# A modulation vector's product moved from matmuls to vector sums, in a three-block model kernel on one Trainium2 core

## The chip, the cores and the metric

The kernel runs on one core of a Trainium2 chip as one program. The metric is the device time of one execution in microseconds (us). The engines spoken of are PE (TensorE, matmuls into PSUM), DVE (VectorE), ACT (ScalarE), POOL (GpSimd) and SP (SyncE, which here only issues the weight loads). Each runs its own queue of instructions in a fixed order and waits on semaphores of the others.

## The reference

All arithmetic is f32: 256 tokens, width 1024. The program is a chain of differential attention, a mixture of 64 experts, latent attention (MLA), another 64 experts, and a last block: a hybrid mixer (window attention "swa", forgetting attention "fox") and a convolutional gated MLP. The last block is modulated by six vectors of a second input `c`:

```python
mod = jax.nn.silu(c) @ w_ada + b_ada            # [1, 1024] @ [1024, 6144]
sh1, sc1, ga1, sh2, sc2, ga2 = jnp.split(mod, 6, axis=-1)
h = modulate(rms_norm_2(x, g_attn), sh1, sc1)   # h * (1 + sc1) + sh1
x = x + ga1[:, None, :] * hybrid_mixer(h, w_in, b_f, sinks, w_out)
h2 = modulate(rms_norm_2(x, g_mlp), sh2, sc2)
x = x + ga2[:, None, :] * conv_glu_mlp(h2, w_up, conv_w, conv_b, w_down)
return rms_norm_2(x, g_final)
```

The change concerns `silu(c) @ w_ada`: one row times 24 MB of weights.

## The kernel before, in words

The stages follow one another: differential attention (0 to 143 us of the profiled span), the first experts (143 to 600), MLA (to about 720), the second experts (to 1262), the mixer (to 1416), the MLP (to 1630). A list scheduler sets the order of every engine's queue when the program is built; SP's order is that of the code, and the experts' PE order is written by hand.

Weights go through 16 **regions** of SBUF (`Regions`), each a 128x2048 f32 tile of 1 MB. `make_plan` lists all loads in order; `fill` issues the next one on SP (L122) whenever a region is free, `done` frees a region after its last reader. So one region that is held longer delays the load that would take its place, and all loads behind it in the queue.

**Modulation.** `cs` (128x8) is silu(c), with k = 0..7 blocks of 128 rows in its columns. `Ada` (class at L429) works through the pieces of a part of `w_ada`. Parts 0 (sh1, sc1) and 1 (ga1, sh2) are 8 pieces of one k block and 2048 columns; parts 4 (sc2) and 5 (ga2) are 4 pieces of two k blocks and 1024 columns. For each k block four matmuls (L444) with a 128x32 broadcast column of `cs` as stationary operand add the four quarters of the columns into the four quadrants of a PSUM tile. These are f32 and each counts as two instructions in the trace: 64 for a part. When the last block is in, `finish` (L453) adds the bias (L462), and transposes (L466) and copies (L471) bring the vector to columns. Part 5 goes another way: ACT copies and POOL adds (L458, L459), and `gate_row` (L481) spreads the row over the partitions.

Part 0 is stepped at the end of differential attention, parts 1 and 4 two pieces at a time beside the mixer's projections qa, qb, kb, vb (`gemm_tok`, L514, through `beside`), part 5 at the end of the mixer's `out_proj` (L552). Its four loads stand in the plan directly behind the four of `w_out`, ahead of the MLP's.

**Around it.** `gemm_tok` and `out_proj` split each weight tile in two (`split`: ACT L399 makes the high part, DVE L400 the low part, 128x1024 each) and `mm3` multiplies in three passes (L415, L416, L417). L416 is the first that needs the low part. While Ada accumulates in PSUM (`ad_ps`), `gemm_tok` with `beside` leaves that tile out (`acc_ps(beside is None)`) and goes through three accumulators. In an attention's pipeline DVE does the score maxima (L586, L588), ACT the exponentials, PE the transposes (L596), and DVE the scaling (L738 in differential attention, L624 in swa). `fence` holds later work back behind the row norms.

Of the kernel before, what the change touches and what calls it, by code (L numbers as in the profile page):

```python
# [18 lines left out]
P = 128  # L19
T = 2  # L20
# [150 lines left out]
def make_plan(a, stop):  # L171
# [5 lines left out]
    def rows(name, w, ncol, k0, nk, c0, nc_):  # L177
        add(name, (nk, nc_), dram(w, k0 * P * ncol + c0, [[ncol, P], [P * ncol, nk], [1, nc_]]))
# [35 lines left out]
    for kh in range(4):  # L214
        rows(("mix_out", kh), a["w_out_2"], 1024, 2 * kh, 2, 0, 1024)
    ada = ada_plan(a, add, (5,))
    for _ in range(4):
        next(ada)
    for i in range(11):
        rows(("up", 0, i), a["w_up_2"], 2 * FF2, 0, 8, 256 * i, 256)  # L220
        rows(("up", 1, i), a["w_up_2"], 2 * FF2, 0, 8, FF2 + 256 * i, 256)
        rows(("down", i), a["w_down_2"], 1024, 2 * i, 2, 0, 1024)
    ends = {1: ("diff_out", 3), 2: ("moe", 0, 15, "d", 3), 3: ("mla_out", 3), 4: ("moe", 1, 15, "d", 3),
            5: ("mix_out", 3)}
    if stop in ends:
# [14 lines left out]
def tile_model(ctx: ExitStack, tc: tile.TileContext, a: dict, out: bass.AP, stop: int = 6):  # L240
# [45 lines left out]
    def acc_ps(four):  # L286

        turn[0] = (turn[0] + 1) % 4
        return ad_ps() if four and turn[0] == 0 else mm_ps()
# [139 lines left out]
    class Ada:  # L429


        def __init__(self, *parts, room=ad_ps):
            self.todo = [(s, pc) for s in parts for pc in ada_pieces(s)]
            self.room = room

        def step(self, n=1):
            for s, (key, k0, nk, _, ncol) in self.todo[:n]:
                if k0 == 0:
                    self.acc = self.room()
                w, m = reg.get(key), ncol // 4  # L440
                with behind_fence():
                    for k in range(nk):
                        for j in range(4):
                            PE.matmul(self.acc[32 * j:32 * j + 32, 0:m],  # L444
                                      lhsT=cs[:, k0 + k:k0 + k + 1].to_broadcast([P, 32]),
                                      rhs=w[:, k, m * j:m * j + m], start=(k0 + k == 0), stop=(k0 + k == 7))
                reg.done(key)
                if k0 + nk == 8:
                    self.finish(s, m)
            self.todo = self.todo[n:]  # L450

# [61 lines left out]

    def gemm_tok(hT, wkeys, ncol, evac, k0=0, beside=None):  # L514

        accs = [acc_ps(beside is None) for _ in range(T)]
        nk = sum(n for _, n in wkeys)
        k = 0
        for key, n in wkeys:
            w = reg.get(key)  # L520
            step = max(1, 1024 // ncol)
            for b in range(0, n, step):
                m = min(step, n - b)
                ws = split(w[:, b:b + m, :])
                for kk in range(m):
                    for t in range(T):
                        mm3(accs[t][:, :ncol], [z[:, k0 + k, ts(t, P)] for z in hT], [z[:, kk, :] for z in ws],
                            k == 0, k == nk - 1)
                    k += 1
            reg.done(key)  # L530
            if beside is not None:
                beside()
        for t in range(T):
            evac(t, accs[t][:, :ncol])

    def out_proj(oT, keys, vec=None):
        accs = token_accs()
        gate = None
        for kp in range(4):
# [8 lines left out]
                        mm3(accs[t][hf], [z[:, k, ts(t, P)] for z in oT], [z[:, ts(hf, 512)] for z in ws],  # L548
                            k == 0, k == 7)
            reg.done(keys[kp])  # L550
        if vec is not None:
            Ada(5, room=sc_ps).step(4)  # L552
        add_to_x(accs, gate)

    def add_to_x(accs, gate=None):
# [878 lines left out]
    def mlp(held):  # L1434
# [35 lines left out]
        def down(j):  # L1470
# [8 lines left out]
                        j == 0, j == NFF - 1)  # L1479
            if j2 == 1:  # L1480
                reg.done(("up", 0, i), ("up", 1, i), ("down", i))
        for j in range(NFF - 1):
            if j >= 2:
                down(j - 2)
            up(j)
        up(NFF - 1)
        for j in range(NFF - 3, NFF):
            down(j)
# [97 lines left out]
```

## Time and profile before

| | |
|---|---|
| median of 3 runs | 1635.39 us (1633.10 to 1638.16) |
| profiled execution, own time | 1631.57 us |
| its span in the trace | 1629.8 us |
| mean granted PE clock | 0.919 of full speed |
| busy: PE, DVE, ACT | 82%, 42%, 27% of the span |
| read from HBM | 508 MB |

The shares are means over stages with different limits, so the rows further down are read by stage: windows give what each engine does in a stretch, the timelines which instruction waits for what. Matmuls are pipelined: one row's time contains the end of the pipeline, and the distance between the starts of rows that follow one another is what an instruction takes from PE. Lines are those of the kernel before; in the changed one most are shifted by 7 to 9.

### The profile page before, as it was taken

The numbers are of one execution on the slowest core, as the hardware profiler recorded it, in microseconds if no ns is written. First come the engines' busy times: TensorE is split into PE (matmuls) and PEld (weight loads), VectorE is DVE, ScalarE is ACT, GpSimd is POOL, SyncE is SP. The second block draws the span as 40 slices with busy tenths as digits, with TensorE's granted clock in tenths as the row PEclk, the third lists the DMA queues.
The fourth block names the chain that finished last, engine by engine and source line by source line (L and its number), as shares of the span: only waits on it lengthen the run. The fifth ranks groups of instructions, "written<-read, shape, count | busy, mean of one in ns | idle before, by whom it ended". The sixth has DMA issues, their size and how long they took to land. (4 is left out here: it accounts for less than half of the span.)

```text
span 1629.8 us, 26706 instructions
## 1 busy us (share of the span) xinstructions
PE 1342.7 (82%) x10695; PEld 927.9 (57%) x10695; DVE 691.8 (42%) x1630; ACT 434.5 (27%) x946; POOL 54.1 (3%) x69
## 2 busy tenths in 40 slices
PE   7998987777677777998877677778777899999996
PEld 6766654443354444776643454545442656599996
DVE  6875232222222223775322222222322754477776
ACT  5764010000000001774000000000001543455555
POOL 2100000000000000120000000000000010000001
PEclk9998999889878899999988989899888999999998
DMA  9377889999999998244999999999899764475410
GB/s 365 127 262 322 334 343 419 419 419 418 417 397 416 418 418 337 93 144 167 392 417 403 418 419 418 419 418 393 341 418 379 285 235 159 149 270 189 171 37 27
DMA packets 112810, 513.14 MB, mean 315 GB/s; under 512 B 13955, under 2 KB 41283, under 8 KB 61344
## 3 DMA queue, kind: packets, MB, share of 16 engines
q1 hardware_dynamic: 111296, 508.14, 78.5%
q8 instruction: 160, 2.62, 0.7%
q0 software_dynamic: 1024, 1.41, 0.3%
q14 instruction: 106, 0.87, 0.1%
q10 hardware_dynamic: 224, 0.10, 0.0%
HBM read 508.56 MB, written 1.05 MB: 313 GB/s over the span
## 5 line engine op out<-in xcount | busy, mean ns | idle before, releaser
L955 PE MATMUL ad<-R,t 128*32 128x256 f32 x4352 | 327.0, 421 | 101.4 <-DMA R<-in_moe_w_up_dram 42.2
L955 PEld LDWEIGHTS ad<-R,t 128*32 128x32 f32 x4352 | 171.1, 120 | 260.3 <-issue 87.6
L910 PE MATMUL sc<-t,R 128*128 128x128 f32 x1120 | 176.1, 323 | 18.2 <-issue 12.0
L910 PEld LDWEIGHTS sc<-t,R 128*128 128x128 f32 x1120 | 167.5, 237 | 20.6 <-issue 17.2
L1007 DVE TENSOR_TENSOR x<-x,mm 128x512 f32<-128x512 f32 x140 | 90.0, 684 | 149.0 <-PE mm L1004 149.0
L982 PE MATMUL mm<-R,t 128*32 128x512 f32 x1120 | 135.4, 625 | 9.5 <-PEq L1047 5.0
L961 ACT ACTIVATE t<-ad 128x256 f32<-128x256 f32 x34 | 13.0, 383 | 481.7 <-PE ad L955 481.7
L963 DVE TENSOR_TENSOR t<-t,ad 128x256 f32<-128x256 f32 x34 | 14.3, 421 | 254.4 <-ACT t L961 254.4
L409 ACT ACTIVATE t<-mm,ws 128x512 fp32r<-128x512 f32 x64 | 44.0, 687 | 263.1 <-PE mm L982 263.1
L912 DVE TENSOR_TENSOR t<-sc,ffng 128x512 f32<-128x512 f32 x70 | 48.4, 692 | 134.6 <-PE sc L910 134.6
L400 DVE TENSOR_TENSOR R<-R,R 128x1024 fp32r<-128x1024 f32 (+3 forms) x78 | 93.2, 1198 | 27.4 <-ACT R L399 26.1
L400 DVE TENSOR_TENSOR t<-R,t 128x1024 fp32r<-128x1024 f32 (+3 forms) x76 | 88.7, 1171 | 23.6 <-ACT t L399 23.4
L410 DVE SCALAR_TENSOR_TENSOR t<-mm,ws,t 128x512 fp32r<-128x512 f32 x64 | 48.0, 751 | 104.3 <-ACT t L409 77.5
L399 ACT ACTIVATE R<-R 128x1024 fp32r<-128x1024 f32 (+3 forms) x78 | 78.7, 1014 | 50.8 <-PE ad L417 15.1
L934 PE MATMUL at<-con,t 128*128 128x128 f32 x70 | 16.6, 323 | 85.5 <-PEq L1083 73.9
L1004 PE MATMUL mm<-t,t 128*128 128x512 f32 x256 | 77.6, 422 | 11.1 <-DVE x L1007 10.2
L399 ACT ACTIVATE t<-R 128x1024 fp32r<-128x1024 f32 (+3 forms) x76 | 76.4, 1008 | 37.8 <-PE ad L416 15.3
L982 PEld LDWEIGHTS mm<-R,t 128*32 128x32 f32 x1120 | 35.0, 114 | 82.9 <-issue 77.5
L1004 PEld LDWEIGHTS mm<-t,t 128*128 128x128 f32 x256 | 43.1, 188 | 45.6 <-DVE x L1007 22.8
L934 PEld LDWEIGHTS at<-con,t 128*128 128x128 f32 x70 | 7.9, 155 | 99.7 <-issue 89.5
L415 PE MATMUL mm<-R,R 128*128 128x512 f32 (+3 forms) x139 | 56.4, 408 | 3.3 <-ACT R L399 2.6
L416 PE MATMUL mm<-R,R 128*128 128x512 f32 (+3 forms) x139 | 55.4, 399 | 0.0
(448 smaller groups left out, 2263.8 us busy)
## 6 DMA issues: line engine op xcount, KB each, us to landing
R<-in_moe_w_gate_dram SPq DMA_DIRECT2D x128, 1024.0 KB, 15.2
R<-in_moe_w_up_dram SPq DMA_DIRECT2D x128, 1024.0 KB, 15.8
R<-in_moe_w_down_dram SPq DMA_DIRECT2D x128, 1024.0 KB, 19.8
R<-in_w_ada_dram SPq DMA_DIRECT2D x24, 1024.0 KB, 7.7
R<-in_w_up_dram SPq DMA_DIRECT2D x22, 1024.0 KB, 6.3
R<-in_diff_w_in_dram SPq DMA_DIRECT2D x12, 1024.0 KB, 15.0
R<-in_w_down_dram SPq DMA_DIRECT2D x11, 1024.0 KB, 5.5
R<-in_w_in_dram SPq DMA_DIRECT2D x8, 1024.0 KB, 7.7
```

Of the source, the lines that this page charges most:

```text
L399: S.activation(hi, w, AF.Copy)
L400: V.tensor_tensor(lo, w, hi.bitcast(F32), op=ALU.subtract)
L409: first = S.activation(hi, src, AF.Copy, scale=scale)
L410: V.scalar_tensor_tensor(lo, src, scale, hi.bitcast(F32), op0=ALU.mult, op1=ALU.subtract)
L415: PE.matmul(acc, lhsT=lt[0], rhs=rt[0], start=start, stop=False, **kw)
L416: PE.matmul(acc, lhsT=lt[0], rhs=rt[1], start=False, stop=False, **kw)
L910: PE.matmul(pg[:, ts(k4, P)], lhsT=h[:, t, 4 * hb + k4, :], rhs=gm[:, t].rearrange("p a b -> p (a b)"), start=(t == 0), stop=(t == 1))
L912: V.tensor_tensor(xg[hb], pg.rearrange("p (k n) -> p k n", k=4), gain[:, 4 * hb:4 * hb + 4, None].to_broadcast([P, 4, P]), op=ALU.mult)
L955: mm = PE.matmul(pgu[32 * j:32 * j + 32, co:co + 256], lhsT=xg[k // 4][:, k % 4, 32 * j:32 * j + 32], rhs=w, start=(k == 0 and co == 0), s ...
L982: mm = PE.matmul(py[32 * j:32 * j + 32, :], lhsT=hT2[:, k, 32 * j:32 * j + 32], rhs=ws[j][:, k, ts(hf, 512)], start=(k == 0), stop=(k == 1))
L1004: PE.matmul(pos[t], lhsT=sc[:, ts(t, P)], rhs=y[part], start=(part == 0), stop=(part == 1))
L1007: V.tensor_tensor(xs, xs, pos[t], op=ALU.add)
```

## The change

For each k block of a part the 128 rows of weights stay in their partitions and are multiplied by the partition's own value of `cs`: ACT copies with a scale for k = 0 (new L447) and DVE adds `weights * cs + sum` for the others (new L449, `scalar_tensor_tensor`, 128x1024, in place into the region of the part's first piece). Where k = 1 stands in the first piece too (parts 4 and 5) it is added from there. After the last block four matmuls (new L455) against a vector of ones add the partitions, into a tile of `sc_ps`. Per 1024 columns that is one ACT copy and seven DVE additions: 42 additions and 6 copies in all. The first piece's region is freed only after these matmuls. `gemm_tok` always goes through four accumulators. Part 5's loads move in the plan behind the MLP's loads i = 1, 3, 5, 7, and its steps into the MLP's loop at j = 3, 7, 11, 15.

```diff
--- before.py
+++ after.py
@@ -214,12 +214,12 @@
     for kh in range(4):
         rows(("mix_out", kh), a["w_out_2"], 1024, 2 * kh, 2, 0, 1024)
     ada = ada_plan(a, add, (5,))
-    for _ in range(4):
-        next(ada)
     for i in range(11):
         rows(("up", 0, i), a["w_up_2"], 2 * FF2, 0, 8, 256 * i, 256)
         rows(("up", 1, i), a["w_up_2"], 2 * FF2, 0, 8, FF2 + 256 * i, 256)
         rows(("down", i), a["w_down_2"], 1024, 2 * i, 2, 0, 1024)
+        if i % 2:
+            next(ada)
     ends = {1: ("diff_out", 3), 2: ("moe", 0, 15, "d", 3), 3: ("mla_out", 3), 4: ("moe", 1, 15, "d", 3),
             5: ("mix_out", 3)}
     if stop in ends:
@@ -429,23 +429,32 @@
     class Ada:
 
 
-        def __init__(self, *parts, room=ad_ps):
+        def __init__(self, *parts):
             self.todo = [(s, pc) for s in parts for pc in ada_pieces(s)]
-            self.room = room
 
         def step(self, n=1):
+
             for s, (key, k0, nk, _, ncol) in self.todo[:n]:
+                w, m = reg.get(key), ncol // 4
                 if k0 == 0:
-                    self.acc = self.room()
-                w, m = reg.get(key), ncol // 4
+                    self.first, self.sums = key, w[:, 0, :]
                 with behind_fence():
                     for k in range(nk):
-                        for j in range(4):
-                            PE.matmul(self.acc[32 * j:32 * j + 32, 0:m],
-                                      lhsT=cs[:, k0 + k:k0 + k + 1].to_broadcast([P, 32]),
-                                      rhs=w[:, k, m * j:m * j + m], start=(k0 + k == 0), stop=(k0 + k == 7))
-                reg.done(key)
+                        by = cs[:, k0 + k:k0 + k + 1]
+                        for c in range(0, ncol, 1024):
+                            part = self.sums[:, c:c + 1024]
+                            if k0 + k == 0:
+                                S.activation(part, part, AF.Copy, scale=by)
+                            else:
+                                V.scalar_tensor_tensor(part, w[:, k, c:c + 1024], by, part, op0=ALU.mult, op1=ALU.add)
+                if k0:
+                    reg.done(key)
                 if k0 + nk == 8:
+                    self.acc = sc_ps()
+                    for j in range(4):
+                        PE.matmul(self.acc[32 * j:32 * j + 32, 0:m], lhsT=one.to_broadcast([P, 32]),
+                                  rhs=self.sums[:, m * j:m * j + m], start=True, stop=True)
+                    reg.done(self.first)
                     self.finish(s, m)
             self.todo = self.todo[n:]
 
@@ -513,7 +522,7 @@
 
     def gemm_tok(hT, wkeys, ncol, evac, k0=0, beside=None):
 
-        accs = [acc_ps(beside is None) for _ in range(T)]
+        accs = [acc_ps(True) for _ in range(T)]
         nk = sum(n for _, n in wkeys)
         k = 0
         for key, n in wkeys:
@@ -548,8 +557,6 @@
                         mm3(accs[t][hf], [z[:, k, ts(t, P)] for z in oT], [z[:, ts(hf, 512)] for z in ws],
                             k == 0, k == 7)
             reg.done(keys[kp])
-        if vec is not None:
-            Ada(5, room=sc_ps).step(4)
         add_to_x(accs, gate)
 
     def add_to_x(accs, gate=None):
@@ -1479,10 +1486,13 @@
                         j == 0, j == NFF - 1)
             if j2 == 1:
                 reg.done(("up", 0, i), ("up", 1, i), ("down", i))
+        ada = Ada(5)
         for j in range(NFF - 1):
             if j >= 2:
                 down(j - 2)
             up(j)
+            if j % 4 == 3:
+                ada.step()
         up(NFF - 1)
         for j in range(NFF - 3, NFF):
             down(j)
```

Three places in the engines' order show what moves. The first is **DVE's queue at the end of differential attention**, where `R_742` is k of the second half of the heads, `R_456` the region of part 0's first piece, and L400 makes the low part of the first `w_out` tile. Before:

```order
178 L691 TENSOR_TENSOR R_742<-R_742,rrk 128x512
179 L410 SCALAR_TENSOR_TENSOR R_461<-at,sub_186,R_460 128x256
180 L691 TENSOR_TENSOR R_742<-R_742,rrk 128x512
181 L586 ISA t_1031,m<-sc,con 128x128
182 L586 ISA m 128x1
...
206 L735 SCALAR_TENSOR_TENSOR rl<-rl,nlam,l 128x2
207 L738 SCALAR_TENSOR_TENSOR t_1067<-t_1068,rl,t_1067 128x128
208 L738 SCALAR_TENSOR_TENSOR t_1067<-t_1068,rl,t_1067 128x256
209 L400 TENSOR_TENSOR R_1376<-R_1015,R_1376 128x1024
```

Of the change:

```order
178 L698 TENSOR_TENSOR R_742<-R_742,rrk 128x512 x2
179 L410 SCALAR_TENSOR_TENSOR R_461<-at,sub_186,R_460 128x256
180 L700 TENSOR_SCALAR qs<-rrq 128x16
181 L702 TENSOR_SCALAR nqs<-rrq 128x16
182 L449 SCALAR_TENSOR_TENSOR R_456<-R_810,cs,R_456 128x1024
183 L449 SCALAR_TENSOR_TENSOR R_456<-R_873,cs,R_456 128x1024 x2
184 L449 SCALAR_TENSOR_TENSOR R_456<-R_907,cs,R_456 128x1024 x2
185 L593 ISA t_1031,m<-sc,con 128x128
...
216 L449 SCALAR_TENSOR_TENSOR R_456<-R_1013,cs,R_456 128x1024
217 L745 SCALAR_TENSOR_TENSOR t_1067<-t_1068,rl,t_1067 128x128
218 L745 SCALAR_TENSOR_TENSOR t_1067<-t_1068,rl,t_1067 128x256
219 L400 TENSOR_TENSOR R_1364<-R_1015,R_1364 128x1024
```

Fourteen additions enter here and a little earlier: three stand before the rows shown, five between the scaling of k and the first score maximum, six between the softmax steps up to the first split of `w_out`.

The second is **PE's queue in the same place**: L725 and L726 (new L732, L733) are scores, the L415 to L417 on `R_1376` (`R_1364` in the change) the first block of the output projection. Before:

```order
368 L725 MATMUL sc<-t_1056,t_1055 128x128
369 L726 MATMUL sc<-t_1056,t_1055 128x256
370 L444 MATMUL ad<-R_776,cs 32x512 x3
371 L444 MATMUL ad<-R_810,cs 32x512 x4
372 L444 MATMUL ad<-R_873,cs 32x512
...
386 L714 MATMUL at<-con,R_742 128x128
387 L444 MATMUL ad<-R_1009,cs 32x512 x3
388 L444 MATMUL ad<-R_1013,cs 32x512 x4
389 L415 MATMUL mm<-R_1376,R_460 128x512
390 L416 MATMUL mm<-R_1376,R_460 128x512
391 L417 MATMUL mm<-R_1376,R_461 128x512
```

Of the change:

```order
368 L732 MATMUL sc<-t_1056,t_1055 128x128
369 L733 MATMUL sc<-t_1056,t_1055 128x256
370 L415 MATMUL mm<-R_1364,R_460 128x512 x3
371 L415 MATMUL ad<-R_1364,R_460 128x512
372 L603 MATMUL at<-con,t_1031 128x128 x3
...
383 L733 MATMUL sc<-t_1119,t_1118 128x256
384 L416 MATMUL mm<-R_1364,R_460 128x512
385 L417 MATMUL mm<-R_1364,R_461 128x512
...
432 L416 MATMUL mm<-t_1413,R_460 128x512
433 L455 MATMUL sc<-R_456,one 32x512 x4
434 L417 MATMUL mm<-t_1412,R_461 128x512
```

The 64 instructions of L444 between scores and projection are gone. Four first passes (L415) stand behind the scores, the first pass with the low part (L416) follows later, and L455 stands in the middle of the projection.

The third is **SP's queue in the mixer**, here with the regions' numbers (R8 is the one of part 1's first piece); "waits" names the engines that are waited for. Before:

```order
948 L122 DMA R8_19912<-in_w_ada_2_dram 128x2048 [waits DMAHW6_49,PE_49]
...
958 L122 DMA R8_20172<-in_w_ada_2_dram 128x2048 [waits DMAHW0_49,PE_49]
...
965 L122 DMA R11_20564<-in_w_in_2_dram 128x4x512 [waits DMAHW7_49,PE_49]
966 L122 DMA R8_20570<-in_w_in_2_dram 128x4x512 [waits DMAHW0_49,PE_49]
967 L122 DMA R7_20616<-in_w_out_2_dram 128x2x1024 [waits DMAHW1_49,DVE_49]
...
970 L122 DMA R1_20671<-in_w_out_2_dram 128x2x1024 [waits DMAHW4_49,DVE_49]
971 L122 DMA R10_20681<-in_w_ada_2_dram 128x2x1024 [waits DMAHW5_49,PE_49]
972 L122 DMA R6_20691<-in_w_ada_2_dram 128x2x1024 [waits DMAHW6_49,PE_49]
973 L122 DMA R11_20738<-in_w_ada_2_dram 128x2x1024 [waits DMAHW7_49,DVE_49]
974 L122 DMA R8_20772<-in_w_ada_2_dram 128x2x1024 [waits DMAHW0_49,DVE_49]
975 L122 DMA R3_20776<-in_w_up_2_dram 128x8x256 [waits DMAHW1_49,PE_49]
```

Of the change:

```order
948 L122 DMA R8_19900<-in_w_ada_2_dram 128x2048 [waits DMAHW6_49,PE_49]
...
958 L122 DMA R7_20157<-in_w_ada_2_dram 128x2048 [waits DMAHW0_49,DVE_49]
...
965 L122 DMA R7_20539<-in_w_in_2_dram 128x4x512 [waits DMAHW0_49,DVE_49]
966 L122 DMA R8_20546<-in_w_in_2_dram 128x4x512 [waits PE_49]
967 L122 DMA R4_20592<-in_w_out_2_dram 128x2x1024 [waits DMAHW1_49,DVE_49]
...
970 L122 DMA R13_20636<-in_w_out_2_dram 128x2x1024 [waits DMAHW5_49,DVE_49]
971 L122 DMA R11_20640<-in_w_up_2_dram 128x8x256 [waits DMAHW6_49,DVE_49]
972 L122 DMA R0_20647<-in_w_up_2_dram 128x8x256 [waits PE_49]
...
976 L122 DMA R14_20734<-in_w_down_2_dram 128x2x1024 [waits DMAHW2_49,PE_49]
977 L122 DMA R2_21022<-in_w_ada_2_dram 128x2x1024 [waits DMAHW3_49,PE_49]
```

The second load of vb (row 966) goes into R8 in both. There R8 had been given back and loaded again once (row 958) before; now it comes from part 1's first piece itself, so the load and the queue behind it wait for L455. The four loads of part 5 behind those of `w_out` are replaced by the MLP's.

## Rows read from the trace of the kernel before

**Rows 1.** Windows from 63 us: length, busy us (instructions) by engine, PE clock, DMA share, GB/s.

```profile
63.00:94.00 31.00, 28.37 (x148) 21.99 (x145) 29.07 (x88) 20.16 (x60) 6.98 (x5) 1.00 0.37 120
...
101.00:112.00 11.00, 10.38 (x83) 3.74 (x75) 8.49 (x31) 9.68 (x28) 0.56 (x1) 1.00 1.02 403
112.00:143.00 31.00, 30.28 (x159) 23.04 (x157) 20.01 (x71) 16.75 (x55) 0.00 (x0) 1.00 0.73 273
143.00:600.00 457.00, 345.21 (x3351) 217.22 (x3350) 122.69 (x286) 40.86 (x75) 0.00 (x0) 0.89 0.98 401
```

**Rows 2.** Timeline of DVE from 90 us: start us, us, line, tiles, [idle before <-releaser].

```profile
100.85 0.29 DVE L586 CUSTOM_DVE_ANT_0 t<-sc,con 128x128 f32<-128x128 f32 x1 [6.52 <-PE sc L726]
...
107.81 2.37 DVE L400 TENSOR_TENSOR R<-R,R 128x1024 fp32r<-128x1024 f32 x2
```

**Rows 3.** Windows of the mixer's start, its middle and the MLP.

```profile
1262.00:1267.00 5.00, 0.27 (x2) 0.00 (x0) 3.00 (x12) 3.77 (x12) 0.00 (x0) 0.78 1.04 365
1267.00:1270.00 3.00, 2.87 (x13) 2.73 (x14) 2.50 (x5) 2.53 (x6) 0.00 (x0) 0.50 0.99 388
1270.00:1274.00 4.00, 4.00 (x28) 3.66 (x29) 4.00 (x11) 1.89 (x5) 0.00 (x0) 0.80 0.76 260
1280.00:1340.00 60.00, 59.92 (x318) 37.83 (x317) 36.84 (x116) 27.77 (x69) 6.56 (x6) 1.00 0.65 243
...
1425.00:1585.00 160.00, 158.25 (x1123) 147.86 (x1123) 119.47 (x177) 91.65 (x134) 0.59 (x1) 1.00 0.50 172
```

**Rows 4.** Timeline of PE from the mixer's end to the MLP's start.

```profile
1416.18 3.66 PE L444 MATMUL sc<-R,cs 128*32 128x256 f32 x64
1423.05 0.66 PE L495 MATMUL at<-con,R 128*128 128x128 f32 x4 [3.21 <-ACT R L1302]
...
1425.11 1.10 PE L481 MATMUL at<-garow,con 128*128 128x256 f32 x4
```

**Rows 5.** Timeline of DVE after the mixer: a 128x1024 operation with one input tensor.

```profile
1422.17 0.75 DVE L1304 TENSOR_SCALAR R<-x,ri_r 128x1024 f32<-128x1024 f32 x1
```

**Rows 6.** DVE groups by form: busy us, mean ns of one, idle before and releasers.

```profile
L400 DVE TENSOR_TENSOR R<-R,R 128x1024 fp32r<-128x1024 f32 x68 | 85.1, 1254 | 25.2 <-ACT R L399 25.0
...
L410 DVE SCALAR_TENSOR_TENSOR t<-mm,ws,t 128x512 fp32r<-128x512 f32 x64 | 48.0, 751 | 104.3 <-ACT t L409 77.5 <-ACTq L1047 26.8
```

**Rows 7.** Windows of line L444 alone: length, its PE busy us (instructions).

```profile
98.00:113.00 15.00, 8.93 (x64) 1.69 (x64) 1.00 0.96 356
1273.00:1280.00 7.00, 4.03 (x26) 0.70 (x26) 1.00 0.66 237
1292.00:1347.00 55.00, 11.67 (x102) 3.11 (x102) 1.00 0.56 208
1416.00:1420.00 4.00, 3.66 (x64) 1.98 (x64) 1.00 1.08 375
```

**Rows 8.** Timeline of PE at the end of differential attention.

```profile
107.09 1.92 PE L444 MATMUL ad<-R,cs 128*32 128x512 f32 x16
108.94 0.49 PE L750 MATMUL at<-R,t 128*128 128x128 f32 x2
...
112.09 0.50 PE L415 MATMUL mm<-R,R 128*128 128x512 f32 x1
112.42 0.39 PE L416 MATMUL mm<-R,R 128*128 128x512 f32 x1
112.65 0.40 PE L417 MATMUL mm<-R,R 128*128 128x512 f32 x1
```

**Rows 9.** Timeline of SP, the loads' queue: first issue us, us, tiles, number.

```profile
1322.16 1.23 SPq L122 DMA_DIRECT2D R<-in_w_in_dram  x2
...
1396.83 0.37 SPq L122 DMA_DIRECT2D R<-in_w_down_dram  x1
```

**Rows 10.** Page, part 6: DMA issues, KB each, median us from issue to landing.

```profile
R<-in_w_in_dram SPq DMA_DIRECT2D x8, 1024.0 KB, 7.7
```

**Rows 11.** Line L1331, the copies out of the projections: DVE's four, first and last start.

```profile
L1331 DVE COPY R<-mm x4: 681/691/692, 1291.9 to 1357.5; 128x512 f32<-128x512 f32 x4
```

## The prediction

> **What bounds the kernel now.** The page's engine shares come first: PE 82%, DVE 42% of the span. These are means over stages with different limits, so I read windows of each stage that the change enters. There the reader is to look for the engine that is full, and for what the others have left.
>
> At the end of differential attention [rows 1] DVE is the limit from 63 to 94 us (29.07 of 31). Around 98 us PE waits for nothing and has nothing urgent: it runs L444 while DVE and ACT do the softmax. From 112 to 143 us PE is full (30.28 of 31). DVE has one gap there, 6.52 us before the first score maximum [rows 2], and 11 - 8.49 = 2.51 us of idle time from 101 to 112. The experts from 143 us on are bound by transfers (DMA share 0.98) [rows 1], so a later end of attention shifts all that follows.
>
> In the mixer PE is the limit: 59.92 of 60 us from 1280 to 1340, with DVE at 36.84 [rows 3]. In the MLP's body, 1425 to 1585, PE is busy 158.25 of 160 us and DVE 119.47 [rows 3]. Between mixer and MLP PE has nothing to do but L444 until the row norm is there: 3.66 us from 1416.18, then 3.21 us idle [rows 4].
>
> **The price of one addition.** No row before shows a two-input multiply-add of 128x1024 from SBUF. One input tensor of that shape costs 0.75 us [rows 5]. Twice a 128x512 multiply-add that reads PSUM is 2 x 0.751 = 1.50 us [rows 6]. The nearest row is L400 with two inputs of the same shape, 1.25 us [rows 6]: I take that, with 0.75 and 1.50 for the range. The Trainium skill bears on this (VectorE: DVE Perf Modes, section "Why `tensor_tensor` can't do 2×_2P or 4×"): the double rate for f32 needs both read ports for one tensor, and a second input occupies one. By it 1.25 stands; were the operation treated as one-input, the 42 additions would take 42 x 0.50 = 21 us less of DVE.
>
> **Part 0, differential attention.** It removes 64 instructions of L444, 8.93 us on PE [rows 7], and adds 14 x 1.25 = 17.5 us on DVE and two ACT copies, which can lie in ACT's idle time before 94 us (20.16 of 31 busy) [rows 1]. PE's saving is worth nothing while the first split of `w_out` is late: that split is at 107.81 on DVE [rows 2], and PE's projection starts at 112.09 [rows 8]. In the new order all 14 additions stand ahead of it. The gap of 6.52 takes five, the slivers of 2.51 two more: 17.5 - 6.52 - 2.51 = 8.5 us remain, so the split starts at 116.3 and ends at 117.5. PE's 30.28 us from 112 to 143 remain, less four first passes that stand ahead of the split's low part (4 x 0.23): 29.4, so the stage ends at 146.9 instead of 143.0, +3.9. DVE's idle 31 - 29.07 = 1.93 us from 63 to 94 could take part of the three early additions, down to +2.0. **I take +3.5.** Bounds: with all additions hidden the projection could start after 107.81 + 1.25 = 109.06 instead of 112.09, -3.0; with the gap alone used, 107.81 + 17.5 - 6.52 + 1.25 + 29.4 = 149.4, +6.4.
>
> **The clock there.** PE loses its filler. Between scores and projection it has a few us of work in some 18. What follows an empty stretch is shown at the mixer's start [rows 3]: PE has 0.27 us of work from 1262 to 1267, then gets 0.50 of the clock (1.2 GHz) for 3 us and 0.80 for 4 us, which loses 3 x 0.5 + 4 x 0.2 = 2.3 us. With the filler the clock was 1.00 from 101 to 112 [rows 1]. **I take +2.3**, between 0 and twice that. The Trainium skill speaks against this change here (TensorE: Matmul & The Clock Gate, section "What's actually happening"): the throttled clock is the default, and only activity releases it, so work that looks idle on PE may hold the clock up. By it the drop comes; without it this term is nothing.
>
> **Parts 1 and 4, mixer.** PE loses 128 instructions: 64 at (108.94 - 107.09)/16 = 0.116 us [rows 8], 7.4 us, and 64 at 3.66/64 = 0.057 us [rows 4], 3.7 us. The 16 new ones (L455) cost 8 x 0.116 + 8 x 0.057 = 1.4. At most 9.7 us are saved. DVE gets 21 x 1.25 = 26.3 us between about 1280 and 1340, where it has 60 - 36.84 = 23.2 idle: 63.1 of 60, so here **DVE becomes the bound**. The additions stand between swa's scalings and the splits for qb, kb and vb, in queue order, so those splits come late and PE waits. In addition vb's second load, issued with the first at 1322.16 [rows 9], now takes the region of part 1's first piece and waits for L455. That stands among kb's matmuls, at about 1341 by my count along PE's queue; with some 5 us to land (7.7 is the median when transfers are crowded) [rows 10] the tile is there at 1346. Its split takes ACT and DVE some 2.5 us for the first half, its 4 x 2 x 3 = 24 matmuls 5.5 us at PE's step of 112.65 - 112.42 = 0.23 [rows 8], so vb's copy, at 1357.5 before [rows 11], comes at about 1355. **I take -2.5.** Bounds: -9.7 if DVE hides everything, +3.1 (63.1 - 60) if it is DVE's sum that counts and PE saves nothing.
>
> **Part 5, MLP.** L444 in the boundary lies in PE's wait for the norm [rows 4], so its removal gains nothing, and the gap of 3.21 us becomes 6.9, longer than the empty stretch at 1262. The clock may fall as there, but half of what follows are transposes paced by ACT and DVE: **+1.2** (0 to 2.3). In the MLP PE gets 8 matmuls (0.5 us), and `gate_row` (1.10 us) [rows 4] moves from the boundary, where it filled part of a wait, into the full body: **+0.8**. Seven additions, 8.8 us, lie beside DVE's 119 of 160; a reason to doubt that is single waits of PE for a low part, at most 4 us. Part 5's four loads leave the place behind `w_out` and the MLP's move up; PE there does not wait for loads, so that is worth nothing. The first of part 5 is the seventh behind `w_out`, where the load of 1396.83 stands now [rows 9]; ACT's copy and one addition wait for it, ahead of the MLP's norm.
>
> **Sum:** 3.5 + 2.3 - 2.5 + 1.2 + 0.8 = +5.3 us on the profiled execution's 1631.57. That execution stands 3.8 under the median of the runs, 1635.39, so I forecast 1635.39 + 5.3 = **1640.7 us**. A measurement of this kernel can tell about 0.3%, 4.9 us, from no change.
>
> **Rivals.**
> 1. *DVE hides the sums and PE's saving is real* (faster). Place: the mixer from 1280 to 1340. It decides where DVE's additions fall only into waits: it needs 26.3 us in 23.2 of idle time, so either an addition costs under 23.2/21 = 1.1 us or some drift past 1340 without holding a split. Against it: they stand ahead of splits in the queue. It gives 0 in attention, -9.7 in the mixer, +0.8: -8.9, 1626.5 us.
> 2. *The clock does not fall*: the score matmuls and first passes keep PE active enough, the boundary too. 3.5 - 2.5 + 0.8 = +1.8, 1637.2 us. For it: 63 to 94 us at 1.00 with PE waiting in places [rows 1]. Against it: the start of the mixer [rows 3].
> 3. *Late regions and a late split*: nothing but the gap hides additions in attention, the mixer goes by DVE's sum, +6.4 + 2.3 + 3.1 + 1.2 + 0.8 = +13.8, 1649.2 us. For it: DVE's order is fixed, and one addition that waits for its load holds the softmax behind it.
>
> **How the numbers follow.** Forecast 0.36, of which 0.05 ends under +4.9; rival 1 0.22; rival 2 0.28; rival 3 0.14. So faster by over 0.3%: 0.22; within: 0.28 + 0.05 = 0.33; slower: 0.31 + 0.14 = 0.45. The range goes from 1628, most of rival 1's side being nearer than its full sum, to 1650, rival 3.
>
> **What would show it.** In the changed profile: L449 near 1.25 us; the first split of `w_out` at 115 to 117 and experts that start 3 to 6 us later; a PE clock under 1 from 112 to 120 and from 1423 to 1430; DVE over 55 of 60 us from 1280 to 1340; vb's second load near 1341 and vb's copy at 1354 to 1356; the MLP's body as long as before. The forecast is wrong if the split stays near 108, if PE's clock holds at 1.00 in both places, or if the fox heads start over 5 us earlier.

## The result: 0.63% slower

| | before | changed |
|---|---|---|
| median of 5 runs each | 1635.39 us (1629.78 to 1638.16) | 1644.46 us (1644.14 to 1648.36) |
| ratio | | 1.0063, 95% interval 1.0038 to 1.0088 |
| profiled execution, own time | 1631.57 us | 1644.14 us |
| its span | 1629.8 us | 1642.4 us |
| mean granted PE clock | 0.919 | 0.906 |

The loss of 9.1 us on the medians was forecast as 5.3, inside the range. The two profiles differ by 12.6 us. I read them by stage, in the order of the prediction.

**End of differential attention.** The windows of the changed kernel, columns as in [rows 1]:

```profile
63.00:94.00 31.00, 29.15 (x152) 22.51 (x151) 30.27 (x91) 21.55 (x65) 6.85 (x5) 1.00 0.39 122
94.00:101.00 7.00, 5.13 (x32) 3.89 (x30) 7.00 (x15) 2.47 (x6) 0.00 (x0) 1.00 0.65 234
101.00:112.00 11.00, 6.85 (x23) 4.69 (x24) 10.88 (x31) 7.57 (x20) 0.56 (x1) 0.51 1.02 400
112.00:120.00 8.00, 7.18 (x29) 5.27 (x29) 5.41 (x19) 3.10 (x11) 0.00 (x0) 0.61 1.05 343
```

DVE is now full from 63 to 112, and PE's clock is 0.51, then 0.61, where it was 1.00. The times of two executions can only be compared from a common point: this execution is already 0.25 us late at the first score maximum of the first half of the heads, which stands ahead of the first addition (52.69 before, 52.94 here). Timeline of DVE, then of PE:

```profile
94.24 6.06 DVE L449 SCALAR_TENSOR_TENSOR R<-R,cs,R 128x1024 f32<-128x1024 f32 x5
100.22 0.28 DVE L593 CUSTOM_DVE_ANT_0 t<-sc,con 128x128 f32<-128x128 f32 x1
...
111.82 1.22 DVE L400 TENSOR_TENSOR R<-R,R 128x1024 fp32r<-128x1024 f32 x1
```

```profile
105.94 1.65 PE L415 MATMUL mm<-R,R 128*128 128x512 f32 x3 [2.83 <-ACT R L399]
...
115.25 0.79 PE L416 MATMUL mm<-R,R 128*128 128x512 f32 x1
```

The first five additions fill exactly the gap that was idle [rows 2], and the score maximum comes no later than before. The first split of `w_out` comes at 111.82 instead of 107.81. PE's matmuls, 0.43 us apart at half clock, start the low part at 115.25. The stage's last add to x starts at 146.53 instead of 143.53; from the common point on that is 2.75 us later, and the split 3.76.

**Mixer.** Windows, columns as in [rows 3], then the waits of PE in the 60 us from 1285 on (engine, line, releaser: us in all, times, longest):

```profile
1280.00:1300.00 20.00, 17.92 (x92) 15.06 (x93) 19.83 (x30) 8.00 (x12) 0.00 (x0) 1.00 0.76 271
1300.00:1320.00 20.00, 16.66 (x82) 11.31 (x81) 18.26 (x46) 9.44 (x20) 3.57 (x3) 1.00 0.86 309
1320.00:1340.00 20.00, 15.78 (x74) 11.12 (x72) 18.49 (x42) 9.29 (x28) 3.06 (x3) 1.00 0.03 8
```

```profile
PE at L603 <- DVE t L631: 3.1, 1, 3.1
PE mm L416 <- DVE t L400: 2.3, 1, 2.3
PE mm L416 <- DVE R L400: 1.3, 1, 1.3
PE at L1376 <- ACT t L605: 1.3, 1, 1.3
PE sc L1389 <- DVE t L1371: 1.1, 1, 1.1
```

DVE is busy 56.6 of 60 us instead of 36.8, PE 50.4 instead of 59.9: the 9.7 us that PE was to save stand there as waits, 9.1 us in these five rows and four of the five for DVE. (The mixer began 4.8 us later here. Counted from 13 us after its first transpose, as in the table further down, DVE has 54.2 and PE 50.9.) The queue of loads (timeline of SP, first issue and the time until the last of the group) shows the second cost:

```profile
1314.73 33.82 SPq L122 DMA_DIRECT2D R<-in_w_in_dram  x2
1348.64 2.36 SPq L122 DMA_DIRECT2D R<-in_w_out_dram  x4
...
1402.68 0.37 SPq L122 DMA_DIRECT2D R<-in_w_ada_dram  x1
```

The second load of vb is issued 33.4 us after the first instead of with it [rows 9], and everything behind it waits too.

**Boundary and MLP.** Timeline of PE:

```profile
1424.19 0.39 PE L417 MATMUL ad<-t,R 128*128 128x512 f32 x1
1430.74 1.11 PE L504 MATMUL at<-con,R 128*128 128x128 f32 x4 [6.16 <-ACT R L1309]
...
1621.93 1.89 PE L490 MATMUL at<-garow,con 128*128 128x256 f32 x8
```

PE's pause is 6.16 us instead of L444 and 3.21 [rows 4]; the spread of the gate row stands in the full part of the MLP. One addition took what was forecast (group by form, mean 1275 ns):

```profile
L449 DVE SCALAR_TENSOR_TENSOR R<-R,cs,R 128x1024 f32<-128x1024 f32 x40 | 50.4, 1275 | 1.1 <-DMA R<-in_w_ada_dram 1.1
```

### The profile page after: what moved, and what is told of

Same layout as the page of the kernel before. It is cut to its first block, busy times and chain, and to the rows that moved or that the text cites. A ratio compares the mean times of both kernels' runs of the same rounds, so it can differ in the third digit from the quotient of the medians.

```text
span 1642.4 us, 26292 instructions
## 1 busy us (share of the span) xinstructions
PE 1336.7 (81%) x10471; PEld 933.5 (57%) x10471; DVE 732.7 (45%) x1672; ACT 439.6 (27%) x952; POOL 54.1 (3%) x69
## 3 DMA queue, kind: packets, MB, share of 16 engines
q0 software_dynamic: 1024, 1.41, 0.3%
## 5 line engine op out<-in xcount | busy, mean ns | idle before, releaser
L962 PE MATMUL ad<-R,t 128*32 128x256 f32 x4352 | 323.5, 419 | 100.4 <-DMA R<-in_moe_w_up_dram 35.9
L962 PEld LDWEIGHTS ad<-R,t 128*32 128x32 f32 x4352 | 166.0, 120 | 261.2 <-issue 96.9
L917 PE MATMUL sc<-t,R 128*128 128x128 f32 x1120 | 182.1, 330 | 14.8 <-issue 8.5
L917 PEld LDWEIGHTS sc<-t,R 128*128 128x128 f32 x1120 | 173.4, 243 | 17.4 <-issue 13.8
L400 DVE TENSOR_TENSOR R<-R,R 128x1024 fp32r<-128x1024 f32 (+3 forms) x78 | 91.8, 1184 | 19.5 <-ACT R L399 18.6
L400 DVE TENSOR_TENSOR t<-R,t 128x1024 fp32r<-128x1024 f32 (+3 forms) x76 | 88.7, 1169 | 16.5 <-ACT t L399 16.2
L1011 PE MATMUL mm<-t,t 128*128 128x512 f32 x256 | 77.7, 423 | 11.0 <-DVE x L1014 10.2
L941 PEld LDWEIGHTS at<-con,t 128*128 128x128 f32 x70 | 8.1, 158 | 101.5 <-issue 89.4
L415 PE MATMUL mm<-R,R 128*128 128x512 f32 (+3 forms) x131 | 53.1, 414 | 7.1 <-ACT R L399 6.4
L416 PE MATMUL mm<-R,R 128*128 128x512 f32 (+3 forms) x131 | 53.6, 409 | 2.4 <-DVE R L400 2.4
```

Of the source, the lines that this page charges most:

```text
L400: V.tensor_tensor(lo, w, hi.bitcast(F32), op=ALU.subtract)
L415: PE.matmul(acc, lhsT=lt[0], rhs=rt[0], start=start, stop=False, **kw)
L416: PE.matmul(acc, lhsT=lt[0], rhs=rt[1], start=False, stop=False, **kw)
L917: PE.matmul(pg[:, ts(k4, P)], lhsT=h[:, t, 4 * hb + k4, :], rhs=gm[:, t].rearrange("p a b -> p (a b)"), start=(t == 0), stop=(t == 1))
L962: mm = PE.matmul(pgu[32 * j:32 * j + 32, co:co + 256], lhsT=xg[k // 4][:, k % 4, 32 * j:32 * j + 32], rhs=w, start=(k == 0 and co == 0), s ...
L1011: PE.matmul(pos[t], lhsT=sc[:, ts(t, P)], rhs=y[part], start=(part == 0), stop=(part == 1))
```

## The experiments

Eleven of the twelve start from the kernel before and get a second class `AdaSum` (the changed `step`) where a part is summed on DVE; fill0 starts from the changed kernel. The diffs leave that class out, and "..." marks other lines left out. Ratios are to the kernel before, with 95% intervals; stage times are of one profiled execution each.

### One part at a time: p0, mix, p5

```diff
p0
-        Ada(0).step(8)
+        AdaSum(0).step(8)
mix
-        ada = Ada(1, 4)
+        ada = AdaSum(1, 4)
-        accs = [acc_ps(beside is None) for _ in range(T)]
+        accs = [acc_ps(True) for _ in range(T)]
p5
+        if i % 2:
+            next(ada)
...
-            Ada(5, room=sc_ps).step(4)
...
+        ada = AdaSum(5)
...
+            if j % 4 == 3:
+                ada.step()
```

> Only part 0 (differential attention) is summed on DVE; parts 1, 4 and 5 as before. Theory 1, late split of w_out and lower clock there: the last add to x in attention at 146.5 instead of 143.5, as in the changed kernel, and the time +3.0 us on the median of before, about 1638.4. Rival: the experts give it back (the stream of weights catches up) and the time is within 1 us of before. Second rival: the 1.8 us that the experts were longer in the changed kernel belong to it as well: +4.8.

> Only parts 1 and 4 (mixer) are summed on DVE; 0 and 5 as before. Theory 1: vb's copy 1.2 us earlier relative to the mixer's start, then the fox heads and the output projection longer, because PE's clock falls there more often than before (10.2 us of clock lost from 1360 to 1416 in the changed kernel, 5.1 before, so about 5 us longer): +2 to +4 us in all. Rival: those falls of the clock are chance, not the change's; then -1 us and the verdict cannot tell it from none. Second rival: DVE is the bound only because part 0 and part 5 shift it: then the gain of PE, up to -9.7, comes out.

> Only part 5 is moved into the MLP and summed on DVE; 0, 1 and 4 as before. Theory 1: PE idle 6.2 instead of 3.2 us ahead of the MLP, clock at 0.50 to 0.62 until some 10 us later, and the MLP's body a little longer: +3 to +4 us. Rival: the transposes behind the norm are paced by ACT and DVE, so the clock costs nothing, and the additions lie in DVE's idle time: within 1 us of before. Second rival: the loads moved away from the place behind w_out free the queue and the time falls by 1 to 3 us.

Measured: p0 1.0030 (1.0016 to 1.0044), mix 1.0007 (0.9988 to 1.0025), p5 1.0010 (0.9989 to 1.0031). The sum, 0.47%, lies in the interval of the whole change, so nothing shows that a part needs another one for its cost; the intervals are too wide to exclude it. Only part 0's loss stands clear of none in the whole time. In p0 the last add to x of attention starts at 145.75, which is 2.55 us later than before from the common point on.

p0 also settles what the 10.2 us of clock are worth that the expectation of mix speaks of, lost between vb's copy and the MLP in the profile of the changed kernel. From the end of attention on, PE's order in p0 is that of the kernel before, and yet its mixer took 155.0 us from the first transpose to the last add to x, against 150.85. The window before the mixer's end, before and in p0, then the two from vb's copy to the last add to x (PE's clock is the third figure from the right):

```profile
1400.00:1416.00 16.00, 16.00 (x69) 10.22 (x67) 5.24 (x21) 7.16 (x17) 0.00 (x0) 1.00 0.34 113
1400.00:1416.00 16.00, 16.00 (x59) 9.83 (x58) 4.97 (x23) 5.99 (x18) 0.00 (x0) 0.79 0.20 67
1357.51:1418.58 61.07, 61.07 (x284) 39.30 (x286) 26.73 (x90) 24.18 (x59) 0.00 (x0) 0.92 0.31 104
1360.77:1426.53 65.76, 65.76 (x285) 41.82 (x287) 26.73 (x90) 24.19 (x59) 0.00 (x0) 0.84 0.28 94
```

The changed kernel had 0.79 in the first of these windows and took 65.8 us at 0.84 in the second. m1 and m4 (further down), whose heads behind vb and output projection are those of the kernel before, took 65.8 us at 0.84 too; p5, whose mixer differs in its loads alone up to the output projection's end, took 61.0 at 0.91, and fill0 (below), which has the mixer of the changed kernel, 61.2 at 0.92. So 4.7 us of the 12.6 between the two profiles are chance, and theory 1 of mix, which gave them to the change, falls. So do the 1.8 us by which experts and MLA were longer: from the last add of attention to the mixer's first transpose the runs took 1120.6 to 1131.0 us, and the code of experts and MLA is the same in all.

### The clock alone: fill0

```diff
+                if s == 0 and k0:
+                    if k0 == 1:
+                        self.idle = ad_ps()
+                    for j in range(4):
+                        PE.matmul(self.idle[32 * j:32 * j + 32, 0:m], lhsT=cs[:, k0:k0 + 1].to_broadcast([P, 32]),
+                                  rhs=w[:, 0, m * j:m * j + m], start=(k0 == 1), stop=(k0 == 7))
                 with behind_fence():
```

> The changed kernel, and PE also gets 56 of the 64 matmul instructions of part 0 back, in the old place between scores and output projection; nobody uses what they add up. DVE's order is that of the changed kernel, word for word. Theory 1 (two costs in attention: DVE's late split and PE's clock): the clock stays at 1.00 from 101 to 120, the last add to x comes at 144.5 to 145.5 instead of 146.5, and the time is 1 to 2.5 us under the changed kernel's, about +7. Rival, the split alone sets it: last add at 146.5, +9. Second rival, the clock alone sets it: last add back at 143.5, +6.

Measured in fill0: windows as above, and the matmuls without a reader in the timeline of PE. Then, from the timelines of DVE, the first score maximum of the first half of the heads (the common point) and the last add to x: before, in the changed kernel and in fill0.

```profile
101.00:112.00 11.00, 9.79 (x79) 4.62 (x71) 10.87 (x34) 7.72 (x21) 0.56 (x1) 1.00 1.02 403
112.00:120.00 8.00, 6.76 (x38) 5.24 (x37) 7.83 (x25) 5.30 (x20) 0.00 (x0) 1.00 0.95 298
```

```profile
98.68 1.04 PE L445 MATMUL ad<-R,cs 128*32 128x512 f32 x2
...
100.51 1.06 PE L445 MATMUL ad<-R,cs 128*32 128x512 f32 x8
...
102.86 5.35 PE L445 MATMUL ad<-R,cs 128*32 128x512 f32 x46
```

```profile
52.69 0.29 DVE L586 CUSTOM_DVE_ANT_0 t<-sc,con 128x128 f32<-128x128 f32 x1 [0.92 <-PE sc L726]
...
143.53 0.69 DVE L560 TENSOR_TENSOR x<-x,ad 128x512 f32<-128x512 f32 x1
```

```profile
52.94 0.29 DVE L593 CUSTOM_DVE_ANT_0 t<-sc,con 128x128 f32<-128x128 f32 x1 [0.92 <-PE sc L733]
...
146.53 0.69 DVE L567 TENSOR_TENSOR x<-x,ad 128x512 f32<-128x512 f32 x1
```

```profile
53.45 0.29 DVE L599 CUSTOM_DVE_ANT_0 t<-sc,con 128x128 f32<-128x128 f32 x1 [0.91 <-PE sc L739]
...
144.29 0.69 DVE L573 TENSOR_TENSOR x<-x,ad 128x512 f32<-128x512 f32 x1
```

From the common point to the last add to x it took 90.84 us before, 93.59 in the changed kernel and 90.84 in fill0. In the ten other runs with part 0 on PE it took 90.8 to 90.9, in p0 93.4. The first split of `w_out` comes as late in fill0 as in the changed kernel, 58.9 us after the same point (52.94 to 111.82, 53.45 to 112.36) instead of 55.1, and yet the stage is as short as before. **Matmuls that nobody reads bring back all of it: the 2.75 us are the clock, and at full clock the late split costs nothing that can be seen.** So it is the second rival, the clock alone, that came out; 144.29 is nearer the 144.5 of theory 1 than the 143.5 of this rival only because this execution stood 0.76 us later already at the first score maximum. The whole time, 1.0050 (1.0032 to 1.0068), cannot tell 3 us from the changed kernel's ratio.

In the changed kernel the clock fell at 101.2 (the window from 101.0 to 101.5 has 0.65, the one from 101.5 to 118.0 has 0.50). In the 7 us ahead of it PE had work for 5.13 us and its longest pause was 1.42 us; in fill0 it had work for 7.00. The Trainium skill (TensorE: Matmul & The Clock Gate, section "What's actually happening") says that the throttled clock is the default and activity releases it; the trace agrees, 0.51 without and 1.00 with the filler. The advice of the Trainium skill (TensorE: Matmul & The Clock Gate, section "Why this matters for your kernels") is about idle gaps between bursts of matmuls; here the only pauses ahead of the fall were 0.45 and 1.42 us long.

### Part 5: the move or the sum, p5pe

Against p5:

```diff
-        ada = AdaSum(5)
+        ada = Ada(5, room=at_ps)
```

> Part 5's loads and steps moved into the MLP as in the change, but its product stays on PE (64 matmul instructions in the MLP's loop instead of 8); parts 0, 1 and 4 as before. Theory 1 (the move costs, not the sum on DVE: PE is full in the MLP and empty at the boundary): the MLP from its first transposes to the end is 3.7 us of matmuls longer than before, plus 1 to 2 us for the spread of the gate row, so +5 to +6, and more than with the sums on DVE. Rival (the seven additions on DVE delay splits in the MLP): then it is shorter than with the sums on DVE, +2 or less.

Measured 1.0024 (1.0007 to 1.0040). By stages, in us, from the timelines of PE:

| | before | p5 | changed | p5pe |
|---|---|---|---|---|
| last add to x to the MLP's first transpose | 5.07 | 4.42 | 4.42 | 4.42 |
| from there to its first product | 3.76 | 4.90 | 4.89 | 5.17 |
| from there to its last product | 189.59 | 192.55 | 193.29 | 194.26 |

Without ACT's and POOL's steps for part 5 the boundary is 0.65 us shorter in all three; it is also 4.4 to 4.5 us in mixswap, best and m1swap, which have these steps, so they are not shown to be the cause. The slower start costs 1.1 us and the MLP's body 3.0 to 3.7. The two lower rows add up to 193.3 to 193.8 us in all ten kernels whose part 5 is as before, and to 197.4 to 199.4 in those with it moved, so this loss is no chance. Steps from one matmul's start to the next, added up over the body, say of what: in p5 the gate row takes 1.5 us instead of 0.5 (before, half of it stood ahead of the first product), the sums over the partitions 0.6, and the products themselves, the same number, 1.4 more (2.1 in the changed kernel), 0.9 of it in steps over 0.3 us. With the product on PE the body takes 1.0 to 1.7 more still. So theory 1 holds: the move costs, by putting into a full PE what was done in its pause, and the sum on DVE is the cheaper way to do it there. What makes the products longer is open: PE's waits in the body are no more than before (1.0 us in p5 and 0.8 in the changed kernel, against 0.8). With the product on PE they take some 0.7 us less than in p5, so that the additions have a share in it, the rival's cause, is likely and not shown. p5's total, 0.10%, is too uncertain to show its 3.5 us alone.

### Why the mixer gains nothing: m1, m4, mixacc, mixswap

```diff
m1
-        ada = Ada(1, 4)
+        ada1, ada4 = AdaSum(1), Ada(4)
...
m4
-        ada = Ada(1, 4)
+        ada1, ada4 = Ada(1), AdaSum(4)
...
mixacc
-        ada = Ada(1, 4)
+        ada = AdaSum(1, 4)
mixswap: as mix, and
-            next(ada)
-            next(ada)
+            if (nm, kh) != ("vb", 0):
+                next(ada)
+            if (nm, kh) != ("kb", 1) and nm != "vb":
+                next(ada)
...
+            turns = iter({"qb": (2, 2), "kb": (2, 1), "vb": (0, 1)}[nm])
...
```

> Only part 1 is summed on DVE (14 additions beside the mixer's projections); parts 0, 4 and 5 as before. Theory 1 (PE's saving in the mixer is given back as waits for DVE's splits once DVE is full): DVE at 36.8 + 18 = 55 of 60 us from 1280 to 1340, PE with 5 to 7 us of waits there, vb's copy within 1 us of before relative to the mixer's start; time -1 to +2. Rival (only the sum of both parts overfills DVE): PE waits under 2 us and vb's copy 4 to 6 us earlier.

> Only part 4 is summed on DVE (7 additions, in the same place); parts 0, 1 and 5 as before. Theory 1: DVE has room for 9 us, so PE's 3.0 us come out: vb's copy 2 to 3 us earlier relative to the mixer's start, time -1 to -3, not to be told from none by the verdict. Rival (any addition ahead of a split holds PE for as long as it lasts): vb's copy as before or later.

> Parts 1 and 4 summed on DVE as in the run of these two parts, but the projections keep their three accumulators (ad left out) as before; parts 0 and 5 as before. Theory 1 (DVE over 54 of 60 us holds the splits): no difference, vb's copy 91 to 93 us after the mixer's first transpose, PE with 8 us of waits in the 60 us. Rival (the fourth accumulator lets the scheduler interleave two projections and that costs): vb's copy at 84 to 87 us, as with one part alone, and time -0.3% and better.

> Parts 1 and 4 summed on DVE with four accumulators, but vb's second load stands ahead of the last piece of part 4 in the plan, so it gets a region that was given back and does not wait for the sums over the partitions; that piece is added beside vb. Theory 2 (the held region is what costs): vb's second load is issued some 10 us or more earlier, vb's copy 4 to 6 us earlier (86 to 88 us after the mixer's first transpose). Theory 1 (DVE full): the load comes early, vb's copy stays at 91 or more, PE's waits for L400 remain.

| | ratio (95%) | DVE, PE busy of the 60 us | PE's clock there | vb's copy after the mixer's first transpose |
|---|---|---|---|---|
| before | 1 | 36.7, 59.9 | 1.00 | 90.4 |
| m4 | 0.9972 (0.9957 to 0.9988) | 44.1, 59.9 | 1.00 | 86.4 |
| m1 | 0.9963 (0.9945 to 0.9980) | 50.1, 57.4 | 1.00 | 85.6 |
| mix | 1.0007 (0.9988 to 1.0025) | 54.3, 51.7 | 0.93 | 92.4 |
| mixacc | 1.0032 (1.0016 to 1.0048) | 54.5, 51.7 | 0.94 | 91.6 |
| mixswap | 1.0019 (1.0005 to 1.0034) | 54.3, 52.5 | 1.00 | 85.3 |

(The 60 us begin 13 us after the first transpose.) **Either part alone brings vb's copy 4 to 5 us earlier; both together gain nothing.** With part 1 alone PE waits little; waits of PE in m1 in these 60 us:

```profile
PE mm L416 <- DVE t L400: 1.5, 1, 1.5
PE mm L416 <- DVE R L400: 0.7, 1, 0.7
PE mm L415 <- DVE R L1363: 0.3, 1, 0.3
```

In m4 the view lists no wait of PE in them at all: DVE has room for 9 us, hardly for 18, and not for 26. The expectation for m1 was off: with DVE at 50 us PE waits 2.5 us, not 5 to 7, and its saving comes out. m4 gained more than was expected, 4.0 us at vb's copy instead of 2 to 3. mixacc rules out the fourth accumulator. What none of the expectations had is the clock: it fell in these 60 us in mix and mixacc, which cost 60 x 0.07 = 4.2 and 60 x 0.06 = 3.6 us of full clock, and not in m1, m4 and mixswap. The changed kernel (0.97, vb's copy at 89.2) and fill0 (0.93, at 91.9) have the mixer code of mix, and their copies differ as the clock does. mixswap takes the held region away; its loads (timeline of SP):

```profile
1308.47 3.35 SPq L122 DMA_DIRECT2D R<-in_w_in_dram  x2
1344.59 0.37 SPq L122 DMA_DIRECT2D R<-in_w_ada_dram  x1
```

vb's second load now goes with the first, and vb's copy comes 7 us earlier than in mix, of which some 4 are the clock, so theory 2 holds for that copy; the load, the PE time behind it and the clock were not tried apart. But PE still waits 7.5 us for DVE in the 60, and the time stays above that of before: the heads behind vb took 3.0 us longer from vb's copy to the last transpose of the fox heads (44.9 against 41.9). In part this is work that only changed its place: part 4's last sum over the partitions now stands behind vb's copy, and 18 of part 5's 64 matmuls, 2.6 us, stand between the products of the output projection. So the held region and DVE's late splits both show as costs, and taking the first away was not enough; that the second alone sets the rest is not shown.

### Versions that might beat both: late4, best, m1swap

```diff
late4
-    ada = ada_plan(a, add, (1, 4))
+    ada = ada_plan(a, add, (1,))
...
-    ada = ada_plan(a, add, (5,))
-    for _ in range(4):
+    ada = ada_plan(a, add, (4, 5))
+    for _ in range(8):
...
-        ada = Ada(1, 4)
+        ada = Ada(1)
...
         reg.give(*hr)
+        ada4 = AdaSum(4)
+        ada4.step(2)
         staged(8, fox_a, None, fox_b)
+        ada4.step(2)
best: late4, and
-        ada = Ada(1)
+        ada = AdaSum(1)
m1swap: m1 with the plan and the turns of mixswap
```

> Only part 4 is summed on DVE, its loads behind those of w_out and its additions beside the fox heads instead of the projections; parts 0, 1 and 5 as before. Theory 1: the projections lose 3.7 us of PE's work and vb's copy comes 3 to 4 us earlier, the additions fall into DVE's idle time of the fox heads (10 of 20 us), time -2 to -3.5 us. Rival: the fox heads are a chain through DVE, each addition of 1.28 us in it costs in full, and the 3 to 4 us are lost again.

> Part 1 summed on DVE beside the projections, part 4 summed on DVE beside the fox heads; parts 0 and 5 as before. The same sums as in the run of both parts, but DVE gets 18 instead of 26 us of them between 1280 and 1340. Theory 1: PE's saving of up to 9.7 us comes out for the most part: vb's copy 82 to 84 us after the mixer's first transpose, time 0.3 to 0.5% under before. Rival (part 4 in the fox heads takes its time back, or the fox heads start early and the gain is lost to the clock): time within 0.2% of before.

> Part 1 alone summed on DVE, as in the run that was 0.37% under before, and vb's second load ahead of the last piece of part 4 in the plan, so that it does not wait for the region of part 1's sums; part 4 stays on PE, its last piece beside vb. Theory 1 with 2 (both costs are taken away: DVE has room, no load waits): vb's second load near 1315 instead of 1346, vb's copy 82 to 85 us after the mixer's first transpose instead of 85.6, time 0.3 to 0.6% under before. Rival (PE is busy to the last microsecond while that load is late, so it costs nothing here): vb's copy at 85 to 86, time as with part 1 alone, -0.2 to -0.5%.

late4: 0.9989 (0.9970 to 1.0009); vb's copy at 86.0, as theory 1 had it, the time not to be told from none. best: 1.0026 (1.0009 to 1.0043), slower, though it was expected to be the fastest; vb's copy at 84.9 instead of 82 to 84. Its additions (line, engine, tiles, count: min, median, max ns, first and last start):

```profile
L493 DVE SCALAR_TENSOR_TENSOR R<-R,cs,R x20: 1259/1275/1285, 1286.8 to 1371.1; 128x1024 f32<-128x1024 f32 x20
```

In best the loads of `w_out` wait behind the region of part 1's sums until 1346.6 (in late4 they were out at 1320.5), part 4's loads stand behind them, and its last addition starts at 1371.1 instead of 1351.6, in the middle of the fox heads; from vb's copy to the last transpose of the fox heads it took 50.7 us, in late4 39.8. That a held region costs through additions that wait for their loads in DVE's queue is what I read from this; it was not tried apart, and much of the difference goes with the clock, which from vb's copy to the last add to x was 0.79 in best and 0.87 in late4 (some 15 of 74.5 us lost against some 8 of 64.2). m1swap: 1.0002 (0.9982 to 1.0021). vb's second load came at 1309, vb's copy at 85.6: PE is full in m1 while the load is late, so the rival was right that it cost nothing there, but its time, that of m1, did not come. The fox heads then took 51.0 us instead of 40.7. From vb's copy to the last add to x, in m1swap and in m1:

```profile
1350.06:1426.24 76.18, 75.38 (x320) 45.98 (x319) 29.74 (x98) 25.21 (x60) 0.72 (x1) 0.78 0.43 150
1359.79:1425.56 65.77, 65.77 (x284) 41.51 (x285) 27.72 (x90) 23.98 (x59) 0.00 (x0) 0.84 0.43 152
```

The clock lost 76.18 x 0.22 = 16.8 us here and 65.77 x 0.16 = 10.5 there: some 6 of the 10.4 us are the clock, and why it fell more often is open.

m1 is the version that beats both kernels: 1631.86 us against 1637.20 of before on the same chip, 0.37% (0.20 to 0.55). It is the best of twelve, and m1swap, the same sums with one load and one piece of part 4 moved, shows no gain.

## Why the prediction was right, and where its terms were off

The direction was right and the time inside the range, but the sum came out near by luck: its term for attention was too large by 3.0 us (3.5 + 2.3 against 2.75) and its gain in the mixer did not come, 2.5 us, while boundary and MLP were too small by 1.5 to 2.2 us. Right as mechanisms were the clock that falls in attention without the matmuls, DVE as the bound of the mixer, the held load, and the slower start of the MLP. Wrong in size was the late split, which was to be the largest cost and cost nothing. The terms:

- *One addition, 1.25 us.* 1.275. Right.
- *The late split in attention, +3.5.* Nothing by fill0: this step was mis-sized. It hid 9.0 us of the 17.5 (the gap and the slivers from 101 to 112). From the common point on the split came 3.76 us later, so some 14 were hidden: the three early additions delayed nothing ahead of 94 (30.27 busy instead of 29.07 from 63 on), and the first score maximum behind them came 0.9 us earlier. So little later, the split costs nothing by the prediction's own path either: in fill0 112.36 + 1.25 + 29.4 = 143.0, where the stage ended before. For before, the projection started only 3.0 us behind the split's end (112.09 against 109.06), and now PE does scores, transposes and four first passes while it waits.
- *The clock there, +2.3.* 2.75 by fill0. The mechanism was right, and the rival of an unchanged clock fell; that the number is near is luck. The windows lose 11 x 0.49 + 8 x 0.39 = 8.5 us of full clock, not 2.3, and two thirds of that did not lengthen the stage.
- *Mixer, -2.5.* In the changed kernel vb's copy came 1.2 us earlier from the first transpose on; mix had it 2.0 later; the time of mix is 0.07% over. DVE as the bound, and vb's held load, were right (forecast for 1341, issued at 1348 in a mixer that began 4.8 later); the gain was smaller than its uncertainty. That the clock falls there too (0.93 in mix) was not in the sum. The rival "DVE hides the sums" holds for one part alone, up to 50 of 60 us.
- *Boundary, +1.2.* 1.1 for the slow start less 0.65 for the shorter boundary.
- *MLP, +0.8.* 3.0 to 3.7: mis-sized. The rows that it names add up to 0.5 + 1.1 = 1.6, and it took half of that without a row; the two took 0.6 + 1.0 = 1.6. What was missing besides are the 1.4 to 2.1 us among the products, which the sum had at nothing; the doubt that it named, waits of PE for a low part of at most 4 us, does not show in PE's waits.

Together 2.75 + 0 + 3.5 to 4.2 is 6.2 to 7.0 us; the measured 9.1 has an interval of 6.2 to 14.4 (0.38% to 0.88% of 1635.4). The remaining 2 to 3 us are open; the 4.7 us by which one kernel's executions differ ahead of the mixer's end are enough for them.

## What to carry to other kernels

Work that fills another engine's pauses is free where it stands: moving it pays only where that engine is full and the new one has room in the same stretch, not in the mean. Count the room window by window: here 18 us of additions in 23 of idle time gained, 26 (with a held load as well) lost it all. Work without urgency on PE can be worth its clock: taking it away cost 2.75 us where a late split of 3.76 us cost nothing. Compare the stages of two profiles from a common point ahead of the change. A sum that is built up in place in a streamed buffer holds that buffer, and the loads behind it, to the end.

## What the runs showed of the hardware that was not expected

- PE's clock fell from 1.00 to 0.50 at 101.2 after 7 us in which PE had work for 5.13 us and no pause over 1.42 us, and stayed there for 17 us; 56 matmul instructions without a reader kept it at 1.00, and the stage was 2.75 us shorter.
- With the same order of PE's instructions the 16 us before the mixer's end got 0.79 in one execution (p0) and 1.00 in another (before). From vb's copy to the last add to x that is 65.8 us at a mean clock of 0.84 against 61.1 at 0.92, so 4.7 us of a difference between two single profiles of this kernel can be of that kind, and stages were compared over several runs.
